# Ten of sixteen output projection blocks in half precision, and three attention pieces that begin one or two ticks later, in a hand-ordered layer kernel

## The chip, the cores and the metric

The kernel runs on one core of one Trainium2 chip. The metric is the device time of one execution in microseconds (us), as the median of several runs. The core has a matrix engine (TensorE, PE in the profile; its weight loads are listed as PEld), a vector engine (VectorE, DVE), an activation engine (ScalarE, ACT), a general engine (GpSimd, POOL), a sync engine (SyncE, SP) that issues most DMAs, an on-chip memory (SBUF) with 128 partitions, and a small memory for products (PSUM).

## The reference

One layer of a streaming encoder handles T = 320 tokens (a prompt of 256, and 64 sample tokens that also see 256 cached ones). The width D is 2048. All data and weights are float32.

```python
xn   = rmsnorm(x, norm_mix)
q, k, v, u, vs, g = split(xn @ w_in)          # 8 heads x 128 each for q, k, v; 1024, 1024; 4096
a    = stick_breaking(q, k, v)                # the sample tokens also see cache_k, cache_v
bb   = gelu(u) * (w_spatial @ rmsnorm(gelu(vs)) + b_spatial)
g_a, g_b = split(sigmoid(g + b_gate))
merged = g_a * (a @ w_branch_a) + g_b * (bb @ w_branch_b)
h    = x + merged @ w_out                     # the output projection, 2048 x 2048
gu   = rmsnorm(h, norm_ffn) @ w_gate_up       # FFN of width 5632
y    = rmsnorm(h + (silu(gu[:, :5632]) * gu[:, 5632:]) @ w_down, norm_final)
```

`stick_breaking` takes scores z = q.k / sqrt(128), forms log sigmoid(-z), sums it from the right along the keys, and weighs the values by exp(log sigmoid(z) + that sum). So each head has scores, a softplus, a scan, an exponential and a second product. The outputs are y and the new k, v and normalised vs.

## The kernel before, in words

Features lie on the partitions: an activation tile is 128 features x 320 tokens, and a matrix is walked in *blocks* of 128 output columns with 16 tiles of 128 inputs each. TensorE does not multiply float32 directly here. Weights and activations are each split into a high and a low part, and `product` (lines 104 to 106) issues three matmuls for each of the 16 tiles: high by high, high by low and low by high. A block is thus 48 matmuls of 320 columns into one PSUM buffer.

There are two ways to split. `Plain` keeps both parts in a 4-byte format (float32r): ScalarE casts the high part (`high`, line 126), VectorE subtracts to get the low part or *rest* (`low`, line 129), in two halves of 1024 columns each. `Group` uses 2-byte parts (float16). Since that format has a small range, the raw block is measured first: `bound` takes for each partition the sum of magnitudes on ScalarE (line 206) or, if the block is named in `by_vector`, the maximum on VectorE (line 202). `pack` (line 214) narrows it, `spread` (line 218) has TensorE broadcast it over partitions into the one `row` PSUM buffer, `close` (lines 222 to 224) takes the peak and makes powers of two `up` and `down`, `high` (line 356) casts raw x up, `low` (line 359) forms the rest, and the product is multiplied by `undo` when it is read. `Acts` does the same for a set of activation tiles: each tile's maximum when it is added, then pack, spread and close one, two and three ticks after the last tile, and from then on three tiles per tick are split by `half` (ScalarE line 166, VectorE line 167 a tick later).

A *tick* is half a block on TensorE. The other engines' steps are put into a table by tick (`at`, `after`) and issued by `rank` within the tick, low ranks first, each time `block` calls `tick`. So the order of instructions on every engine but GpSimd is what this table makes of it; each engine works its list strictly in that order. Before a block that starts at tick s, a `Plain` loads at s-8 and s-7, casts at s-2 and s-1, and takes the rests at s-1 and s. A `Group` (lead 11) loads at s-11 and s-10, bounds at s-8 (rank 4), packs at s-7 (rank 3), spreads at s-5 and closes at s-4 (rank 1), casts at s-3 and takes the rest at s-2 (rank 2). There are 5 raw buffers and 3 split buffers of one block each.

The stages are, in order: a start whose first heads are computed as the weights arrive; 6 `Plain` blocks (heads); then `line`, the list of half precision groups (4 gates, the other 12 heads, 8 blocks vs, 8 blocks u, 6 gates, and 16 branch blocks "ab" with gates between); the output projection `outs`, 16 `Plain` blocks that read the merged tiles as float32r pairs `mh`, `ml`; and the FFN, whose first three gate/up pairs (6 blocks) are `Plain` and all others `Group`. While the output projection runs, each finished block is added to x (`residual`, line 1021), multiplied by the norm's gain and split (`gained`, lines 159 and 160), and squared on ScalarE (line 275) and summed on GpSimd (line 276). The FFN's own half precision input comes from `Features`: `measure`, `spread` and `close` bound the gains during the output projection, and `normed` multiplies two tiles per tick by the norm's factor, each then split by `half`.

Attention works on four *pieces* of two heads. `attend(p, now)` puts one piece's steps into the table, over 19 ticks: parts now+1, planes +2, scores +3 and +4 (TensorE), gathering +4 and +5, softplus +6 and +7, scan +8 and +9, exponential +10 and +11, transposing DMAs +13, joining +16 (`together`, line 581, with the rests of line 601 a tick later), and the second product `att_out` +19 (TensorE). The rests of `att_parts` and `att_past` (lines 601 and 616) are what the scores read. GpSimd takes some of them.

## Time and profile before

| | us |
|---|---|
| median of 3 runs | 1622.87 |
| the three runs | 1621.71, 1622.87, 1623.84 |
| profiled execution | 1620.54 |
| its span (first to last instruction) | 1618.7 |
| start and first heads, up to the first half precision block | 0 to 90.94 |
| half precision: heads, gates, branches | 90.94 to 624.83 |
| output projection | 624.83 to 737.69 |
| FFN and end | 737.69 to 1618.7 |

A busy share tells how much of the span an engine works, averaged over stages with different limits; which engine ends last is read stage by stage. A row of the waits gives the waiting engine, what it was about to make (tile and line), what it waited for, the total in us, the number of times, and the longest. A row of the windows gives a stretch of time, its length, then busy time with the number of instructions for the engine, and the clock granted to TensorE as a share of full speed (PEclk).

### The profile page before, as it was taken

How to read it: one execution, taken by the hardware profiler on the slowest of the kernel's cores; microseconds unless marked ns; L12 is line 12 of the kernel's file. 1: busy time of each engine (PE TensorE's matmuls, PEld its weight loads, DVE VectorE, ACT ScalarE, POOL GpSimd, SP SyncE). 2: the span in 40 equal slices, each digit the busy share in tenths (PEclk: the TensorE clock that was granted, in tenths of full speed). 3: DMA queues.
4: the chain of work that ended last, by engine and by line, in shares of the span. 5: the costliest groups of instructions: out<-in, count | busy, mean ns of one | idle time of the engine just before them, and what ended most of it. 6: DMA issues, size and time to landing. Idle time of an engine off the chain costs nothing.

```text
span 1618.7 us, 28003 instructions
## 1 busy us (share of the span) xinstructions
PE 1598.7 (99%) x11692; PEld 1225.4 (76%) x11692; DVE 1089.1 (67%) x1819; ACT 1004.5 (62%) x1119; POOL 65.3 (4%) x80
## 2 busy tenths in 40 slices
PE   9989999999999999999999999999999999999997
PEld 9967777777777778999777777777777777777775
DVE  6788987886566565547856568665555776555775
ACT  6578999768666653446665656445555754565662
POOL 0110112100000000111000000000000000000000
PEclk9999999999999999999999999999999999999999
DMA  8656765554444444557544444444444444444321
GB/s 302 206 165 197 218 184 152 168 165 164 167 159 156 157 159 154 170 170 247 182 157 157 156 158 166 167 168 169 162 157 157 156 156 157 159 164 144 134 79 65
DMA packets 100511, 268.34 MB, mean 166 GB/s; under 512 B 28992, under 2 KB 35392, under 8 KB 100384
## 3 DMA queue, kind: packets, MB, share of 16 engines
q1 hardware_dynamic: 97936, 261.36, 48.4%
q0 software_dynamic: 1312, 3.80, 0.7%
q8 instruction: 91, 1.49, 0.4%
q10 hardware_dynamic: 1136, 1.39, 0.2%
q14 instruction: 36, 0.29, 0.0%
HBM read 256.03 MB, written 5.51 MB: 162 GB/s over the span
## 4 chain that ended last, share of the span: by engine, by line
PE 86%; ACT 6%; DVE 5%; issue 2%; DMA 1%; SPq 0%; DVEq 0%; ACTq 0%
PE acc L105 27%; PE acc L104 27%; PE acc L106 27%; PE aux L451 2%; ACT w L356 1%; ACT junk L206 1%; DVE w L359 1%; DMA raw<-w_in 1%; DVE tops L202 1%; PE acc L451 1%; DVE half L167 1%; DVE w L129 0%; PE row L218 0%; DMA turned<-wp 0%; DVE wt L581 0%
## 5 line engine op out<-in xcount | busy, mean ns | idle before, releaser
L105 PE MATMUL acc<-half,w 128*128 128x320 f16 x3232 | 967.1, 299 | 1.0 <-DVE half L167 1.0
L104 PE MATMUL acc<-half,w 128*128 128x320 f16 x3232 | 967.3, 299 | 0.0
L106 PE MATMUL acc<-half,w 128*128 128x320 f16 x3232 | 967.1, 299 | 0.1
L356 ACT ACTIVATE w<-raw,up 128x2048 f16<-128x2048 f32 (+1 forms) x206 | 405.4, 1968 | 449.1 <-PE acc L106 440.0
L359 DVE SCALAR_TENSOR_TENSOR w<-raw,up,w 128x2048 f16<-128x2048 f32 (+1 forms) x206 | 474.9, 2305 | 182.9 <-ACT w L356 182.8
L106 PEld LDWEIGHTS <-w 128*128 128x128 f16 x3232 | 316.4, 98 | 124.7 <-issue 1.2
L104 PEld LDWEIGHTS <-w 128*128 128x128 f16 x3232 | 316.5, 98 | 124.3 <-issue 1.3
L105 PEld LDWEIGHTS <-w 128*128 128x128 f16 x3232 | 316.5, 98 | 117.7 <-issue 0.2
L206 ACT ACTIVATE junk<-raw 128x2048 uint8<-128x2048 f32 (+1 forms) x149 | 278.0, 1866 | 1.7 <-DMA raw<-w_in 1.7
L222 DVE TENSOR_REDUCE peak<-row 128x1 f32<-128x128 f32 x148 | 42.6, 288 | 182.3 <-PE row L218 182.2
L202 DVE TENSOR_REDUCE tops<-raw 128x1 f32<-128x2048 f32 (+1 forms) x57 | 127.7, 2240 | 0.5 <-DMA raw<-w_gu 0.5
L126 ACT CAST w<-raw 128x1024 fp32r<-128x1024 f32 x56 | 58.7, 1048 | 94.2 <-PE acc L106 78.2
L129 DVE TENSOR_TENSOR w<-raw,w 128x1024 fp32r<-128x1024 f32 x56 | 68.8, 1232 | 50.3 <-ACT w L126 50.3
L104 PE MATMUL acc<-mh,w 128*128 128x320 f32 x256 | 79.3, 310 | 0.0
L105 PE MATMUL acc<-ml,w 128*128 128x320 f32 x256 | 79.1, 309 | 0.0
L106 PE MATMUL acc<-mh,w 128*128 128x320 f32 x256 | 79.1, 309 | 0.0
L104 PEld LDWEIGHTS acc<-mh,w 128*128 128x128 f32 x256 | 48.1, 188 | 0.0
L105 PEld LDWEIGHTS acc<-ml,w 128*128 128x128 f32 x256 | 48.1, 188 | 0.0
L106 PEld LDWEIGHTS acc<-mh,w 128*128 128x128 f32 x256 | 48.0, 188 | 0.0
L104 PE MATMUL acc<-S,w 128*128 128x320 f32 x144 | 44.7, 310 | 0.0
L106 PE MATMUL acc<-S,w 128*128 128x320 f32 x144 | 44.5, 309 | 0.0
L105 PE MATMUL acc<-S,w 128*128 128x320 f32 x144 | 44.5, 309 | 0.0
(227 smaller groups left out, 1197.7 us busy)
## 6 DMA issues: line engine op xcount, KB each, us to landing
raw<-w_gu SPq DMA_DIRECT2D x176, 512.0 KB, 5.7
raw<-w_in SPq DMA_DIRECT2D x141, 512.0 KB, 4.8
raw<-w_down SPq DMA_DIRECT2D x80, 512.0 KB, 4.9
raw<-w_out SPq DMA_DIRECT2D x32, 512.0 KB, 4.1
raw<-w_a SPq DMA_DIRECT2D x16, 512.0 KB, 3.7
raw<-w_b SPq DMA_DIRECT2D x16, 512.0 KB, 4.7
raw<-w_down SPq DMA_DIRECT2D x16, 256.0 KB, 4.5
x<-xT SPq DMA_DIRECT2D x8, 320.0 KB, 7.8
```

The source lines that it names most:

```text
L104: nc.tensor.matmul(ps[:, :T], a, x[0], start=first, stop=False, skip_group_check=True)
L105: nc.tensor.matmul(ps[:, :T], a, x[1], start=False, stop=False, skip_group_check=True)
L106: nc.tensor.matmul(ps[:, :T], b, x[0], start=False, stop=last, skip_group_check=True)
L126: nc.scalar.copy(out=self.w[j][0], in_=self.raw[:, j * HALF * P : (j + 1) * HALF * P])
L129: nc.vector.tensor_tensor(out=self.w[j][1], in0=self.raw[:, j * HALF * P : (j + 1) * HALF * P], in1=self.w[j][0].bitcast(F32), op=ALU.subt ...
L167: after(1, lambda: nc.vector.scalar_tensor_tensor(out=x[:, 1], in0=src, scalar=factor, in1=x[:, 0], op0=ALU.mult, op1=ALU.subtract), rank=3)
L202: nc.vector.tensor_reduce(out=self.tops[:, i : i + 1], in_=src, axis=mybir.AxisListType.X, op=ALU.max, apply_absolute_value=True)
L206: nc.scalar.activation(out=junk, in_=src, func=AF.Abs, accum_out=self.tops[:, i : i + 1])
L222: nc.vector.tensor_reduce(out=top, in_=self.row[:, :P], axis=mybir.AxisListType.X, op=ALU.max)
L356: nc.scalar.activation(out=w[:, 0], in_=self.raw[u][:, : self.width[u]], func=AF.Copy, scale=self.scale.up)
L359: nc.vector.scalar_tensor_tensor(out=self.w[u][1], in0=self.raw.pop(u)[:, : self.width[u]], scalar=self.scale.up, in1=self.w[u][0], op0=AL ...
L451: nc.tensor.matmul(first[b][h][:, :T], w[:, (h * n + j) * P : (h * n + j + 1) * P], xs[c + j][i], start=not last and c + j + i == 0, stop= ...
```

## The change

The output projection's first 6 blocks stay `Plain`. Blocks 6 to 15 become `Group`s with lead 11: weights bounded (on VectorE where m%3 is 2, so three of the ten), and the merged tiles collected in a new set `whole = Acts(KD)`, so that each merged tile's maximum is taken as it is merged, and 16 tiles are split into float16 pairs at ticks 3 to 8 of the stage. The float32r pairs are still made. `residual` of those blocks multiplies by `undo` on the way.

`attend` begins two ticks later for pieces 0 and 1, one later for piece 2, and at the same tick for piece 3. The step `att_past`, which is put into the table apart from `attend`, stays where it was.

Which blocks of `line` are bounded by VectorE follows a new rule: none of the first four, from 4 to 32 those whose number leaves 1 or 3 when divided by 5, then none up to 40, and then every third. Before, it was every third throughout (by the column block for "in", by m for "ab"). In the FFN the first groups are no longer bounded by VectorE (`made > 6`).

Closings (`Group.close`, `Acts.close`, and the FFN's `Features.close`, which also moves from tick 8 to tick 7 of the output projection) get rank 0.5, ahead of the other steps of their tick but the loads. The FFN's `normed` steps are spread over 7 ticks instead of 8.

```diff
+WHOLE_OUT = 6
...
-            at(last + 7, self.close, late_undo, rank=1)
+            at(last + 7, self.close, late_undo, rank=0.5)
...
-                at(now + 3, self.close, rank=1)
+                at(now + 3, self.close, rank=0.5)
...
-    attend(0, base + 10)
+    attend(0, base + 12)
...
+        by_vector = (0,) if 4 <= i < 33 and i % 5 in (1, 3) or i > 40 and i % 3 == 2 else ()
         if kind == "in":
-            g = Group([[(w_in[n][:, j * HALF * P : (j + 1) * HALF * P], HALF) for j in range(2)]], start, lambda: [mixed.undo], 11,
-                      (0,) if i % 3 == 2 else ())
+            g = Group([[(w_in[n][:, j * HALF * P : (j + 1) * HALF * P], HALF) for j in range(2)]], start, lambda: [mixed.undo], 11, by_vector)
         else:
-            g = Group([[(w_a[n], H), (w_b[n], H)]], start, lambda: [aT.undo, bT.undo], 11, (0,) if n % 3 == 2 else (), True)
+            g = Group([[(w_a[n], H), (w_b[n], H)]], start, lambda: [aT.undo, bT.undo], 11, by_vector, True)
...
-    outs = [Plain(w_out[m], KD, out_start + 2 * m) for m in range(KD)]
+    whole = Acts(KD)
+    outs = [Plain(w_out[m], KD, out_start + 2 * m) for m in range(WHOLE_OUT)]
+    outs += [Group([[(w_out[m][:, j * HALF * P : (j + 1) * HALF * P], HALF) for j in range(2)]], out_start + 2 * m,
+                   lambda: [whole.undo], 11, (0,) if m % 3 == 2 else (), True) for m in range(WHOLE_OUT, KD)]
...
-            attend(1, state["tick"] + 9)
+            attend(1, state["tick"] + 11)
         elif name == "v" and h % 2:
-            attend(h // 2, state["tick"] + 1)
+            attend(h // 2, state["tick"] + (2 if h == 5 else 1))
...
+        whole.add(t)
...
-                groups[kind, s, i] = Group([pieces(w_gu[i], 0, KD), pieces(w_gu[KF + i], 0, KD)], now, lambda: [ffn.undo], min(14, now - ffn_start), (1,) if made % 2 else ())
+                groups[kind, s, i] = Group([pieces(w_gu[i], 0, KD), pieces(w_gu[KF + i], 0, KD)], now, lambda: [ffn.undo], min(14, now - ffn_start), (1,) if made % 2 and made > 6 else ())
...
-    at(out_start + 8, ffn.close)
+    at(out_start + 7, ffn.close, rank=0.5)
...
-        nc.vector.tensor_tensor(out=hs[m], in0=ps, in1=x, op=ALU.add)
+        if m < WHOLE_OUT:
+            nc.vector.tensor_tensor(out=hs[m], in0=ps, in1=x, op=ALU.add)
+        else:
+            nc.vector.scalar_tensor_tensor(out=hs[m], in0=ps, scalar=outs[m].undo, in1=x, op0=ALU.mult, op1=ALU.add)
...
-        ps = outs[m].block(merged)
+        ps = outs[m].block(merged) if m < WHOLE_OUT else outs[m].block(0, whole.half)
...
-        at(base + 3 + m // 2, lambda m=m: ffn.normed(m, hs[m], "rh", lambda: rooms["raw"].tile([P, T], F32, tag="normed", bufs=6, name="normed")))
+        at(base + 3 + 7 * m // 16, lambda m=m: ffn.normed(m, hs[m], "rh", lambda: rooms["raw"].tile([P, T], F32, tag="normed", bufs=6, name="normed")))
```

Line numbers after the change are one higher up to about line 800 and more behind it. The order of the engines' lists shows the moves. First VectorE at the scores of piece 0, where `S<-q` and `S<-k` are the rests that the scores read (the last is `128x2x64`, line 616 before and 617 after), `w<-raw,up,w` is a weight block's rest, and `peak`, `down`, `up`, `undo` are a closing. Before:

```order
L222 TENSOR_REDUCE peak<-row 128x1
L223 TENSOR_TENSOR down<-peak,bits 128x1
L224 TENSOR_TENSOR up<-down,bits 128x1
L349 TENSOR_SCALAR undo<-down,undo_610 128x1
L359 SCALAR_TENSOR_TENSOR w<-raw,up,w 128x2048
L601 TENSOR_TENSOR S<-q,S 128x256
L601 TENSOR_TENSOR S<-k,S 128x256 x2
L616 TENSOR_TENSOR S<-q,S 128x2x64
L757 TENSOR_TENSOR v<-acc,rx 128x320
```

After, the same place:

```order
L360 SCALAR_TENSOR_TENSOR w<-raw,up,w 128x2048
L758 TENSOR_TENSOR v<-acc,rx 128x320
L215 TENSOR_SCALAR packed<-tops 128x1
L223 TENSOR_REDUCE peak<-row 128x1
L224 TENSOR_TENSOR down<-peak,bits 128x1
L225 TENSOR_TENSOR up<-down,bits 128x1
L350 TENSOR_SCALAR undo<-down,undo_610 128x1
L360 SCALAR_TENSOR_TENSOR w<-raw,up,w 128x2048
L602 TENSOR_TENSOR S<-q,S 128x256
L602 TENSOR_TENSOR S<-k,S 128x256 x2
L617 TENSOR_TENSOR S<-q,S 128x2x64
```

The rests of piece 0 now stand behind one more closing and one more weight rest, and behind the reading of a head v that followed them before.

On GpSimd, the three subtractions of piece 0's cached keys (`S<-k,S 128x320 x3`) and a memset of 512 columns stand like this before:

```order
L759 DMA k_t<-k 128x320
L528 MEMSET wso 128x512
L535 DMA wso<-ws_t 64x4x64 x2
L601 TENSOR_TENSOR S<-k,S 128x320 x3
L759 DMA v_t<-v 128x320
```

And after:

```order
L760 DMA k_t<-k 128x320
L602 TENSOR_TENSOR S<-k,S 128x320 x3
L529 MEMSET wso 128x512
L536 DMA wso<-ws_t 64x4x64 x2
L760 DMA v_t<-v 128x320
```

The subtractions come ahead of the memset.

Second, VectorE where piece 2 is joined (`wt<-turned`) and the scores of piece 3 are gathered (`z<-aux,mdiag`). Before:

```order
L581 COPY wt<-turned 128x2x640
L581 COPY wt<-turned 128x2x512
L222 TENSOR_REDUCE peak<-row 128x1
L223 TENSOR_TENSOR down<-peak,bits 128x1
L224 TENSOR_TENSOR up<-down,bits 128x1
L349 TENSOR_SCALAR undo<-down,undo_610 128x1
L359 SCALAR_TENSOR_TENSOR w<-raw,up,w 128x2048
L202 TENSOR_REDUCE tops<-raw 128x1
L658 TENSOR_TENSOR z_2883<-aux,mdiag 128x2x128
```

After:

```order
L223 TENSOR_REDUCE peak<-row 128x1
L224 TENSOR_TENSOR down<-peak,bits 128x1
L225 TENSOR_TENSOR up<-down,bits 128x1
L350 TENSOR_SCALAR undo<-down,undo_610 128x1
L360 SCALAR_TENSOR_TENSOR w<-raw,up,w 128x2048
L203 TENSOR_REDUCE tops<-raw 128x1
L582 COPY wt<-turned 128x2x640
L582 COPY wt<-turned 128x2x512
L659 TENSOR_TENSOR z_2881<-aux,mdiag 128x2x128
```

The joining of piece 2 has come to stand in the same tick as the gathering for piece 3 and directly ahead of it.

Third, VectorE in the output projection around the fifth and sixth tick, where `w<-raw,w 128x1024` is half a `Plain` block's rest, `h<-acc,ev` a residual and `S<-h,gain,S` a gained rest. Before:

```order
L129 TENSOR_TENSOR w<-raw,w 128x1024
L1021 TENSOR_TENSOR h<-acc,ev 128x320
L160 SCALAR_TENSOR_TENSOR S<-h,gain,S 128x320
L129 TENSOR_TENSOR w<-raw,w 128x1024 x2
L1021 TENSOR_TENSOR h<-acc,ev 128x320
L160 SCALAR_TENSOR_TENSOR S<-h,gain,S 128x320
```

After:

```order
L130 TENSOR_TENSOR w<-raw,w 128x1024
L1027 TENSOR_TENSOR h<-acc,ev 128x320
L215 TENSOR_SCALAR packed<-tops 128x1
L168 SCALAR_TENSOR_TENSOR half<-gate,act_up,half 128x320 x3
L161 SCALAR_TENSOR_TENSOR S<-h,gain,S 128x320
L223 TENSOR_REDUCE peak<-row 128x1
L224 TENSOR_TENSOR down<-peak,bits 128x1
L225 TENSOR_TENSOR up<-down,bits 128x1
L130 TENSOR_TENSOR w<-raw,w 128x1024
L168 SCALAR_TENSOR_TENSOR half<-gate,act_up,half 128x320 x3
L203 TENSOR_REDUCE tops<-raw 128x1
```

Between two residuals there are now the rests of three merged tiles per tick, a closing and, once, a block's maximum.

## The prediction

> **What bounds the kernel now.** I read the page's first two parts, then busy time by windows for TensorE, then its waits, then the groups of instructions by line and shape, and last the timeline around each wait.
>
> ```profile
> span 1618.7 us, 28003 instructions
> PE 1598.7 (99%) x11692; PEld 1225.4 (76%) x11692; DVE 1089.1 (67%) x1819; ACT 1004.5 (62%) x1119; POOL 65.3 (4%) x80
> ```
>
> TensorE (PE) is busy 99% of the span, so time can only come from a faster matmul or from its few waits. The windows below are, in order: the 16 output projection blocks; 30 plain half precision blocks (gates and branches); two blocks with the scores of attention piece 1 in them; one block with the output of piece 0; the block that holds the scores of piece 0; the five blocks in which piece 3 ends; the first half precision block of the FFN.
>
> ```profile
> core 0: us, PE busy (x), PEclk, DMA share, GB/s
> 624.83:737.69 112.86, 112.86 (x771) 1.00 0.53 166
> 408.10:605.37 197.27, 197.27 (x1472) 1.00 0.47 161
> 132.72:147.69 14.97, 14.97 (x115) 1.00 0.98 245
> 154.26:163.18 8.92, 8.92 (x72) 1.00 0.35 118
> 90.94:106.40 15.46, 10.40 (x65) 0.78 0.64 194
> 256.87:297.16 40.29, 37.44 (x268) 0.96 0.64 180
> 780.18:788.01 7.83, 6.87 (x51) 1.00 0.28 107
> ```
>
> A float32r block takes 112.86/16 = 7.05 us, a half precision one 197.27/30 = 6.58 us (its bound's broadcast matmul included), so a tick (half a block) is 3.52 or 3.29 us. Scores add 14.97 - 2 x 6.58 = 1.8 us, an output piece 8.92 - 6.58 = 2.3 us. What is left over is waiting:
>
> - **A**, scores of piece 0: 15.46 - 6.58 - 1.8 = 7.1 us
> - **B**, end of piece 3: 40.29 - 5 x 6.58 - 2.3 = 5.1 us
> - **C**, start of the FFN: 7.83 - 6.58 = 1.25 us
>
> ```profile
> PE aux L629 <- DVE S L616: 5.1, 1, 5.1
> PE row L218 <- DVE peak L222: 1.5, 3, 0.8
> PE aux L721 <- DVE S L601: 1.3, 1, 1.3
> PE acc L105 <- DVE half L167: 1.0, 1, 1.0
> PE aux L721 <- ACT S L600: 0.6, 1, 0.6
> ```
>
> These are TensorE's own waits (us in total, times, longest): A is the first, B the 1.3, the 0.6 and half of the 1.5, C the 1.0. Everywhere else the other engines' waiting costs nothing.
>
> **The change, part by part: attention.** Around A the timeline shows VectorE (DVE), GpSimd (POOL) and TensorE:
>
> ```profile
> 92.74 3.11 DVE L224 TENSOR_TENSOR up<-down,bits 128x1 int32<-128x1 int32 x1
> 95.89 2.33 DVE L359 SCALAR_TENSOR_TENSOR w<-raw,up,w 128x2048 f16<-128x2048 f32 x1
> 99.16 0.28 DVE L616 TENSOR_TENSOR S<-q,S 128x128 fp32r<-128x128 f32 x1
> ...
> 93.32 2.50 POOL L601 TENSOR_TENSOR S<-k,S 128x320 fp32r<-128x320 f32 x3
> ...
> 102.34 0.47 PE L104 MATMUL acc<-half,w 128*128 128x320 f16 x1
> 102.61 0.47 PE L105 MATMUL acc<-half,w 128*128 128x320 f16 x1
> 103.34 0.30 PE L105 MATMUL acc<-half,w 128*128 128x320 f16 x1
> 103.48 0.30 PE L106 MATMUL acc<-half,w 128*128 128x320 f16 x1
> ```
>
> TensorE stood until 99.4, when the last rest of piece 0 was done; the matmuls after it start 0.27 us apart instead of 0.14 until 103.3, which is part of the 7.1. Without the wait the scores would have begun at 99.4 - 5.1 = 94.3; two ticks later that is 94.3 + 2 x 3.29 = 100.9. VectorE has one weight rest (2.3), one closing of a bound and two small steps more before that point, some 3.5 us, and, since group 2's bound goes to ScalarE (ACT), one reduction of 2.3 us less, of which up to all is lost waiting for ScalarE. So the rest is ready between 99.4 + 3.5 - 2.3 = 100.6 and 102.9: a wait of 0 to 2.0 us, and no slow clock. I take 0.8, nearer the lower end, because the 3.11 us step (0.18 us as a rule, by its row further down) goes with GpSimd's three subtractions, which now come ahead of their memset and so fall earlier. A gains 6.3.
>
> B is different, for there ScalarE is the bound. Windows from the gathering of piece 2 to that of piece 3, and on to the end of piece 3 (PE, PEld, DVE, ACT, POOL):
>
> ```profile
> 191.31:234.87 43.56, 43.56 (x331) 32.54 (x329) 35.87 (x71) 40.93 (x54) 4.10 (x6) 1.00 0.72 196
> 234.87:290.17 55.30, 52.45 (x385) 38.81 (x383) 43.37 (x80) 48.72 (x61) 14.43 (x8) 0.98 0.53 152
> ```
>
> ScalarE works 40.9 of 43.6 us. Pieces 0 and 1 start two ticks later, piece 2 one, piece 3 at the same tick: from 1 to 2 and from 2 to 3 it is now 11 ticks instead of 12. A tick less takes 3.3 us of time away and only about 1.9 us of ScalarE's work (half a high part of 2.0 us, half of 0.6 bounds at 1.9 and a readout, 0.3 for reading a product), so each interval loses 1.4 us of slack. The removed A gives nothing here; it was TensorE's slack. Also the joining of piece 2 now stands ahead of the gathering for piece 3 in the same tick:
>
> ```profile
> L581 DVE COPY wt<-turned 128x1280 uint16<-128x1280 uint16 x4 | 3.6, 891 | 0.0
> L581 DVE COPY wt<-turned 128x1024 uint16<-128x1024 uint16 x4 | 3.0, 738 | 0.0
> ```
>
> That is 1.6 us of VectorE. Against that, the bound at the tick of group 28 moves from ScalarE to VectorE (2.1 us off the engine that is late), and group 29's goes the other way. So B becomes 5.1 - 2.0 = 3.1 at best, 5.1 + 2 x 1.4 + 1.6 = 9.5 at worst; I take 6.5, one interval's loss. A and B together: 12.2 - 0.8 - 6.5 = **4.9 gained**, between 0.7 (2.0 and 9.5 left) and 9.1 (0 and 3.1 left).
>
> **Output projection.** Ten blocks go from 7.05 to 6.58: 10 x 0.478 = 4.8 us, less one broadcast matmul for the bound of the merged tiles (under 0.1): 4.7. Prices of what is added, from the groups by shape (busy us, mean ns):
>
> ```profile
> L359 DVE SCALAR_TENSOR_TENSOR w<-raw,up,w 128x2048 f16<-128x2048 f32 x190 | 445.9, 2347 | 178.0 <-ACT w L356 178.0
> L356 ACT ACTIVATE w<-raw,up 128x2048 f16<-128x2048 f32 x190 | 380.2, 2001 | 416.1 <-PE acc L106 407.0 <-PE row L218 2.5 <-DVE undo L349 2.5
> L206 ACT ACTIVATE junk<-raw 128x2048 uint8<-128x2048 f32 x137 | 260.4, 1901 | 1.7 <-DMA raw<-w_in 1.7
> L202 DVE TENSOR_REDUCE tops<-raw 128x1 f32<-128x2048 f32 x53 | 120.7, 2277 | 0.5 <-DMA raw<-w_gu 0.5
> L129 DVE TENSOR_TENSOR w<-raw,w 128x1024 fp32r<-128x1024 f32 x56 | 68.8, 1232 | 50.3 <-ACT w L126 50.3
> L126 ACT CAST w<-raw 128x1024 fp32r<-128x1024 f32 x56 | 58.7, 1048 | 94.2 <-PE acc L106 78.2 <-issue 10.4 <-PE aux L451 4.9
> L167 DVE SCALAR_TENSOR_TENSOR half<-act,act_up,half 128x320 f16<-128x320 f32 x44 | 21.5, 544 | 0.0
> L276 POOL TENSOR_TENSOR sq_h<-sq_h,sq 128x320 f32<-128x320 f32 x14 | 14.8, 1061 | 389.9 <-ACT sq L275 389.9
> L160 DVE SCALAR_TENSOR_TENSOR S<-h,gain,S 128x320 fp32r<-128x320 f32 x16 | 11.7, 739 | 5.5 <-ACT S L159 5.5
> L160 DVE SCALAR_TENSOR_TENSOR S<-x,gain,S 128x320 fp32r<-128x320 f32 x8 | 4.1, 548 | 4.7 <-ACT S L159 4.6
> L224 DVE TENSOR_TENSOR up<-down,bits 128x1 int32<-128x1 int32 x148 | 26.5, 179 | 5.1
> L222 DVE TENSOR_REDUCE peak<-row 128x1 f32<-128x128 f32 x148 | 42.6, 288 | 182.3 <-PE row L218 182.2
> ```
>
> Splitting costs no more than before (one high part of 2.0 us for two casts of 1.05, one rest of 2.35 for two of 1.23). New are ten bounds (seven on ScalarE at 1.9 and a readout that I put at 0.2, three on VectorE at 2.3) and 16 merged tiles' halves and rests. In the later blocks this is hidden: ScalarE 2.0 + 2.1 + 1.0 and VectorE 2.35 + 0.8 + 1.3 lie under 6.58. The full place is ticks 3 to 8 of the stage, 6 x 3.52 = 21.1 us. VectorE has there six weight rests (7.4), 15 halves' rests (8.2), three closings (2.6), three residuals (at a half's rest) and two gained rests (3.1), a reduction for block 8 (2.3), packings (0.6): 24.2. ScalarE has six casts (6.3), 16 high halves (about as long as their rests, 8.7), two bounds (4.2), three pairs of gained and square (1.0 each): 22.2. The next weight rest must be done 7 ticks after the start, at 24.6, and would end at 24.2 + 1.2 = 25.4. The 30 or so rows overlap their neighbours by up to 0.06 us each, which could bring it down to 23.6. So TensorE waits 0 to 0.8 there; VectorE being late also delays the closing of a bound that a broadcast waits for, and a raw buffer that is asked for one tick before it is free. I take 1.0, bounds 0 to 3. Net **3.7 gained**, between 1.7 and 4.7.
>
> The longer matmul hides nothing now: in half precision a block leaves 0.47 us less to the engines beside it, which is in the 6.58 already.
>
> Here a rule speaks against the change. GpSimd adds one square per block; rests beside it took 739 instead of 548 ns, 0.19 us more. The Trainium skill (SBUF — State Buffer, section "SBUF: two separate sides") says that VectorE and GpSimd share a port pair as an exclusive lock, and whoever starts second is blocked for the whole instruction; the 3.11 us step at 92.74 agrees. By it the three adds of those six ticks would cost VectorE up to 3.2 us instead of 0.6.
>
> **FFN.** All normalised tiles are ready one tick earlier, and two reductions (4.6 us) leave VectorE for ScalarE before C. VectorE's list up to the last rest shrinks from about 31 to 27 us, while the wait was 1.25. ScalarE gets 4.2 us in two ticks with slack around them. C gains **1.2**, bounds 0 and 1.25. Closing bounds ahead of equal work in a tick moves steps of 0.2 to 0.8 us within VectorE's queue; I cost it at nothing, with 0.7 either way (the remaining 0.7 of the waits for the peak).
>
> **The rivals.**
>
> 1. Attention's waits go altogether: the bound moved off ScalarE at piece 3 is enough and A fits. Gain 12.2 + 3.7 + 1.2 = 17.1, 1605.8 us. Against it stand the 94% of ScalarE. Chance 0.12.
> 2. GpSimd's adds hold VectorE for their whole length in the output projection: 24.2 + 3.2 + 1.2 = 28.6 against 24.6, a wait of 4.0 instead of 1.0. Gain 9.8 - 3.0 = 6.8, 1616.1 us. For it speaks one step of 3.11, against it the 739. This is the lock rule's case. Chance 0.08.
> 3. Half precision is no faster there, or the blocks are fed too late throughout: gain 4.9 + 1.2 - 1.0 = 5.1, 1617.8 us. The 30 blocks speak against it. Chance 0.05.
> 4. Slower: the squeezed pieces do not shrink with the ticks, because their steps wait for each other. A rest of piece 1 (then 2) now stands on VectorE behind the maximum of the next piece, which waits for ScalarE's logarithm:
>
> ```profile
> DVE e L672 <- ACT e L667: 9.1, 4, 2.8
> ```
>
> Then both lost ticks come back as waits (6.6), both outputs wait 2.8, and each long wait brings the slow clock of A again (1.8 each): B is 5.1 + 6.6 + 5.6 + 3.6 = 20.9, A 2.0, so 10.7 lost against 4.9 gained elsewhere: 1628.7 us. It decides from B over 18 us on. Chance 0.06.
>
> My own case has 0.69.
>
> **How the numbers follow.** 4.9 + 3.7 + 1.2 = 9.8 us. The profiled execution took 1620.5 us (span 1618.7) and would take 1610.7; the median of the runs is 1622.9, 2.4 above it, and all differences come from gaps that do not depend on that, so I predict 1622.9 - 9.8 = **1613.1 us**. My case alone reaches from a gain of 15.1 (9.1 + 4.7 + 1.25) to one of 2.4 (0.7 + 1.7 + 0): 1607.8 to 1620.5. The range, with most of rival 1, is 1606 to 1620.5. A change under 0.2%, 3.2 us, can't be told from none here. My case falls short of that in about one of 20, rival 3 in one of five: faster 0.87, same 0.07, slower 0.06.
>
> **What would show it.** Output blocks 6 to 15 at 6.58 us and a wait under 1 us near the sixth; TensorE's wait at L616's successor under 2.0 us with the clock at 1.00; the wait for the rests of piece 3 still there, 3 to 9 us with ScalarE over 90% busy; none on the halves at the FFN. I am wrong if B goes to nothing or over 10, or if TensorE waits over 3 us in the output projection.

## The result, and the profile after

The changed kernel takes 1610.52 us (median of 6 runs, 1610.40 to 1612.64) against 1623.36 (median of 6, 1621.71 to 1624.23): a ratio of 0.9924, 95% interval 0.9911 to 0.9936. It is faster by 12.8 us. The forecast was 1613.1, with a range of 1606 to 1620.5. One execution of the kernel before, beside the later experiments, took 2790.15 us at a mean granted clock of 0.556, and no number below uses it.

The two profiled executions differ by less, 1620.54 and 1610.42 us (spans 1618.7 and 1608.6): 10.1 us. The remaining 2.7 us are taken up further down. The page of the changed kernel:

```profile
span 1608.6 us, 28118 instructions
PE 1591.9 (99%) x11703; PEld 1201.1 (75%) x11703; DVE 1126.9 (70%) x1905; ACT 1016.0 (63%) x1131; POOL 68.1 (4%) x80
```

TensorE is still the bound, so the question is again which of its waits went and which came. Its waits now (total, times, longest):

```profile
PE aux L630 <- DVE S L617: 1.6, 1, 1.6
PE row L219 <- DVE peak L223: 1.3, 3, 0.5
PE aux L722 <- DVE S L602: 1.1, 1, 1.1
PE acc L107 <- DVE w L360: 1.1, 1, 1.1
PE acc L105 <- DVE ev L1063: 1.0, 1, 1.0
```

The first two rows look like old waits that shrank. The first is not: it stands before the scores of another piece. Windows cut at the same blocks show where the 10.1 us come from. First the kernel before, in this order: the block with the scores of piece 0 and the next; the two blocks with the scores of piece 2; the seven blocks around the end of piece 3; the last eight branch blocks; the output projection; the FFN's six plain blocks; the six behind them.

```profile
90.94:112.99 22.05, 16.99 (x114) 0.85 0.59 174
176.33:191.31 14.98, 14.98 (x114) 1.00 1.03 304
256.87:310.74 53.87, 50.81 (x367) 0.97 0.65 181
572.49:624.83 52.34, 52.34 (x392) 1.00 0.44 145
624.83:737.69 112.86, 112.86 (x771) 1.00 0.53 166
737.69:780.18 42.49, 42.49 (x293) 1.00 0.79 265
780.18:820.72 40.54, 39.58 (x293) 1.00 0.51 177
```

The same blocks of the changed kernel:

```profile
90.68:105.65 14.97, 14.97 (x115) 1.00 0.62 207
169.00:185.82 16.82, 15.17 (x115) 1.00 1.00 247
251.46:302.37 50.91, 49.24 (x367) 1.00 0.68 190
564.12:619.08 54.96, 53.14 (x391) 1.00 0.42 139
619.08:727.56 108.48, 108.48 (x783) 1.00 0.55 175
727.56:771.31 43.75, 42.77 (x292) 1.00 0.69 242
771.31:810.61 39.30, 39.30 (x293) 1.00 0.55 193
```

Length is the first number behind the stretch. Gained: 7.1 at the scores of piece 0, 3.0 at the end of piece 3, 4.4 in the output projection, 1.2 at the FFN's first half precision block. Lost: 1.8 at the scores of piece 2, 2.6 in the last branch blocks, 1.3 in the FFN's plain blocks. With 0.3 us from the start the sum is 10.2, against 10.1 of the spans; all other stretches agree within 0.1.

### The profile page after: what moved, and what is told of

It is laid out like the page before. It is cut to its first block, busy times and chain, and to the rows that moved or that the text cites. A ratio compares the mean times of both kernels' runs of the same rounds, so it can differ in the third digit from the quotient of the medians.

```text
span 1608.6 us, 28118 instructions
## 1 busy us (share of the span) xinstructions
PE 1591.9 (99%) x11703; PEld 1201.1 (75%) x11703; DVE 1126.9 (70%) x1905; ACT 1016.0 (63%) x1131; POOL 68.1 (4%) x80
## 4 chain that ended last, share of the span: by engine, by line
PE 90%; ACT 5%; DVE 3%; issue 1%; DMA 0%; DVEq 0%; POOL 0%; ACTq 0%
PE acc L105 29%; PE acc L107 29%; PE acc L106 29%; PE aux L452 2%; ACT w L357 1%; PE acc L452 1%; DVE w L360 1%; ACT junk L207 1%; DVE tops L203 1%; PE row L219 1%; DMA bsb<-bs 0%; ACT S L601 0%; ACT L667 0%; DVE h L1179 0%; PE row L416 0%
## 5 line engine op out<-in xcount | busy, mean ns | idle before, releaser
L107 PE MATMUL acc<-half,w 128*128 128x320 f16 x3392 | 1014.2, 299 | 1.2 <-DVE w L360 1.1
L105 PE MATMUL acc<-half,w 128*128 128x320 f16 x3392 | 1014.3, 299 | 0.4 <-DVE gate L967 0.3
L106 PE MATMUL acc<-half,w 128*128 128x320 f16 x3392 | 1014.2, 299 | 0.0
L357 ACT ACTIVATE w<-raw,up 128x2048 f16<-128x2048 f32 (+1 forms) x216 | 425.3, 1969 | 470.8 <-PE acc L107 465.8
L360 DVE SCALAR_TENSOR_TENSOR w<-raw,up,w 128x2048 f16<-128x2048 f32 (+1 forms) x216 | 499.0, 2310 | 190.8 <-ACT w L357 190.8
L107 PEld LDWEIGHTS <-w 128*128 128x128 f16 x3392 | 331.9, 98 | 130.6 <-DVE w L360 1.8
L105 PEld LDWEIGHTS <-w 128*128 128x128 f16 x3392 | 331.9, 98 | 130.5 <-issue 1.5
L106 PEld LDWEIGHTS <-w 128*128 128x128 f16 x3392 | 331.9, 98 | 123.7 <-issue 0.9
L127 ACT CAST w<-raw 128x1024 fp32r<-128x1024 f32 x36 | 37.6, 1044 | 41.1 <-PE acc L107 29.5
L130 DVE TENSOR_TENSOR w<-raw,w 128x1024 fp32r<-128x1024 f32 x36 | 44.4, 1235 | 4.0 <-ACT w L127 3.9
L1078 DVE SCALAR_TENSOR_TENSOR h<-acc,undo,h 128x320 f32<-128x320 f32 x47 | 25.7, 547 | 16.2 <-PE acc L107 16.2
L219 PE MATMUL row<-turner,packed 128*128 128x128 bf16 x159 | 34.9, 220 | 1.4 <-DVE peak L223 1.3
L277 POOL TENSOR_TENSOR sq_h<-sq_h,sq 128x320 f32<-128x320 f32 x14 | 18.1, 1290 | 385.6 <-ACT sq L276 385.6
L105 PE MATMUL acc<-mh,w 128*128 128x320 f32 x96 | 30.2, 315 | 0.0
```

The costliest lines, as they stand in the source:

```text
L105: nc.tensor.matmul(ps[:, :T], a, x[0], start=first, stop=False, skip_group_check=True)
L106: nc.tensor.matmul(ps[:, :T], a, x[1], start=False, stop=False, skip_group_check=True)
L107: nc.tensor.matmul(ps[:, :T], b, x[0], start=False, stop=last, skip_group_check=True)
L127: nc.scalar.copy(out=self.w[j][0], in_=self.raw[:, j * HALF * P : (j + 1) * HALF * P])
L130: nc.vector.tensor_tensor(out=self.w[j][1], in0=self.raw[:, j * HALF * P : (j + 1) * HALF * P], in1=self.w[j][0].bitcast(F32), op=ALU.subt ...
L219: nc.tensor.matmul(self.row[:, :P], self.own.to_broadcast([P, P]), turner, start=True, stop=True)
```

## The experiments

Twelve kernels gave a time, nearly all of them the changed kernel with one part undone. A thirteenth, with all three edits at the FFN's start undone together (first bounds, closing of the gains, normalised tiles), deadlocks and has no time. "Scores of piece 0", "end of piece 3" and so on are the stretches above. Each stretch is read from one profile per kernel, and the medians are given beside it.

**Attention's pieces at their old ticks.**

```diff
-    attend(0, base + 12)
+    attend(0, base + 10)
...
-            attend(1, state["tick"] + 11)
+            attend(1, state["tick"] + 9)
...
-            attend(h // 2, state["tick"] + (2 if h == 5 else 1))
+            attend(h // 2, state["tick"] + 1)
```

> The changed kernel with attention's pieces begun at the old ticks, all else as changed. If the scores of piece 0 gained by beginning later (my theory), their block takes 13 to 15.5 us again instead of 8.4: 5 to 7 us lost; the new wait before the scores of piece 2 (1.8 us) goes, since the maximum that stands before their rests falls behind them. If the gain at the end of piece 3 (2.9 us) comes from which engine takes the bounds, it stays here, and the sum is 1610.5 + 7.1 - 1.8 = about 1615.8 us. Rival: the pieces' new spacing made that gain; then another 2.9 is lost, about 1618.7 us.

Measured: 1617.15 us (1615.98 to 1619.97). The scores of piece 0 take 21.4 us again, those of piece 2 15.0 without a wait, the end of piece 3 49.8, even 1.1 less than in the changed kernel. But 2.6 us are lost between, among them a new wait of 1.5 us before the scores of piece 3. The gain at the end of piece 3 does not come from the spacing.

**The old choice of bounds on VectorE.** The code of this edit also shows that the old choice went by a group's place in `line` (by m for "ab"), not by the column block. The groups are numbered by that place.

```diff
-        by_vector = (0,) if 4 <= i < 33 and i % 5 in (1, 3) or i > 40 and i % 3 == 2 else ()
+        by_vector = (0,) if (i if kind == "in" else n) % 3 == 2 else ()
```

> The changed kernel with the old choice of blocks of the line that VectorE bounds, all else as changed. By my theory ScalarE is late again at the end of piece 3, with the pieces closer together: 2.9 us or more lost there (up to 7, as the prediction's 9.5 us of waiting would have it); the scores of piece 2 lose their new wait of 1.8; the scores of piece 0 keep their gain but for 0 to 2 us; the branch blocks keep their 2.6 us of waiting, because that hangs on a buffer and not on VectorE's load. Sum: 1611 to 1617 us. Rival: the branch blocks wait because VectorE now bounds most of them; then those 2.6 us go here, and the sum is 2.6 less.

Measured: 1619.7 us (1617.5 to 1621.2), above what I expected. The branch blocks keep their 2.6 us, as expected. The end of piece 3 takes 52.7, so 1.8 are lost there. But the scores of piece 0 take 19.3 us and those of piece 2 19.0: I had expected at most 2 us lost at the first, and a gain at the second. VectorE at piece 0, where TensorE waits for line 617:

```profile
97.55 2.34 DVE L360 SCALAR_TENSOR_TENSOR w<-raw,up,w 128x2048 f16<-128x2048 f32 x1
99.81 2.28 DVE L203 TENSOR_REDUCE tops<-raw 128x1 f32<-128x2048 f32 x1
102.00 0.41 DVE L602 TENSOR_TENSOR S<-q,S 128x256 fp32r<-128x256 f32 x1
102.34 0.75 DVE L602 TENSOR_TENSOR S<-k,S 128x256 fp32r<-128x256 f32 x2
103.01 0.28 DVE L617 TENSOR_TENSOR S<-q,S 128x128 fp32r<-128x128 f32 x1
```

The maximum of line 203 is that of group 5. With the old choice it falls in the same tick as the rests and is ranked ahead of them.

**The same, with the rests ahead of a maximum.** The old choice as above, and the rests for the scores get rank 3.5 instead of 5 (a bound has 4). `parts` gets an argument `rank=5` for it, and uses it for its rest.

```diff
-        s["qp"] = parts(s["q"][:, :, P:TP])
-        s["kp"] = [parts(s["k"][:, j, 0:TP]) for j in range(2)]
+        s["qp"] = parts(s["q"][:, :, P:TP], rank=3.5)
+        s["kp"] = [parts(s["k"][:, j, 0:TP], rank=3.5) for j in range(2)]
...
-        after(1, lambda: nc.vector.tensor_tensor(out=own[:, :, 1], in0=new, in1=own[:, :, 0].bitcast(F32), op=ALU.subtract))
+        after(1, lambda: nc.vector.tensor_tensor(out=own[:, :, 1], in0=new, in1=own[:, :, 0].bitcast(F32), op=ALU.subtract), rank=3.5)
```

> The changed kernel with the old choice of bounds on VectorE, and with the rests for the scores put ahead of a block's maximum in the same tick. With the old choice alone the scores' blocks took 12.7 us (piece 0) and 12.4 us (piece 2). Theory: at piece 0 TensorE waits because one maximum of 2.3 us (group 5's) stands right before the rests; ahead of it they are ready 2.3 us earlier, and without the long wait the slow matmuls go too: 8.4 to 9.3 us, some 3.5 to 4.3 gained. At piece 2 no maximum stands there; ScalarE is late with two bounds in a row, and the block stays at 12 to 12.6 us. Sum: 1619.7 - 4 = about 1615.7 us. Rival: at both places it is the load of VectorE and ScalarE that counts and not the order; then both blocks change by under 1 us, 1619 us or above.

Measured: 1615.81 us (1615.29 to 1618.41), as expected. VectorE at the same place:

```profile
99.76 0.42 DVE L602 TENSOR_TENSOR S<-q,S 128x256 fp32r<-128x256 f32 x1
100.10 0.75 DVE L602 TENSOR_TENSOR S<-k,S 128x256 fp32r<-128x256 f32 x2
100.77 0.28 DVE L617 TENSOR_TENSOR S<-q,S 128x128 fp32r<-128x128 f32 x1
100.97 2.27 DVE L203 TENSOR_REDUCE tops<-raw 128x1 f32<-128x2048 f32 x1
```

The same work in another order: the rests end 2.2 us earlier, and the block takes 8.8 us instead of 12.7. At piece 2, where no maximum stands ahead and VectorE waits 2.5 us for a cast of ScalarE just before the rests, nothing changes (12.4).

**Both old.** The pieces at their old ticks and the old choice of bounds together; the rests keep their rank.

> The changed kernel with both the pieces' old starts and the old choice of bounds on VectorE. It completes a table of four: from the first half precision block to the end of piece 3 (29 blocks) the kernel before took 219.9 us, the changed one 211.7, with the old starts 218.0, with the old choice 220.4. Theory: these two edits alone make the 8.1 us, and only together; closings moved ahead count for nothing there. Then it takes 219.9 us: 1610.5 + 8.1 = 1618.6 us. Rival: the closings' new rank made part of it; then the stretch takes 216 to 219 us, 1615 to 1617.5 us.

Measured: 1620.84 us (1618.45 to 1623.49), profiled 1620.02. That is 2.2 us above the forecast in the median. The 29 blocks take 221.0 us, 1.2 more than before the change; 0.9 of it are at piece 0, after the same long wait. So the closings' rank alone does not make the gain, and the table of four is:

| 29 blocks, us | old choice of bounds | new choice |
|---|---|---|
| old starts | 221.0 | 217.9 |
| later starts | 220.3 | 211.7 |

Later starts alone gain 0.6, the choice alone 3.1, both 9.3. By the medians of the whole kernels the same steps are 1.1, 3.7 and 10.3.

**The closings' old rank.**

```diff
-            at(last + 7, self.close, late_undo, rank=0.5)
+            at(last + 7, self.close, late_undo, rank=1)
...
-                at(now + 3, self.close, rank=0.5)
+                at(now + 3, self.close, rank=1)
```

> The changed kernel with the closings of groups and of activation sets at their old rank, all else as changed. Theory: steps of 0.2 to 0.8 us within VectorE's queue, nothing: 1610.5 us within 0.7, as the prediction has it. Rival: without them a broadcast waits longer for its peak where VectorE is busiest, at piece 3 and at the branch blocks' end: 1 to 2 us lost, 1611.5 to 1612.5 us.

Measured: 1610.57 us (1610.39 to 1610.76). No difference, as the prediction had it.

**Other buffers for three gates.** The new waits in the branch blocks hang on ScalarE. Its list in the changed kernel:

```profile
564.32 2.00 ACT L357 ACTIVATE w<-raw,up 128x2048 f16<-128x2048 f32 x1 [1.91 <-PE acc L107]
578.31 0.53 ACT L840 ACTIVATE gate<-acc,undo 128x320 f32<-128x320 f32 x1 [11.99 <-PE acc L107]
578.74 1.90 ACT L207 ACTIVATE junk<-raw 128x2048 uint8<-128x2048 f32 x1
...
581.53 3.88 ACT L357 ACTIVATE w<-raw,up 128x2048 f16<-128x2048 f32 x2
```

A gate's reading waits 12 us "for PE acc". The product that it reads was done at 564.1, when its block ended, so the wait is for something else that TensorE releases. The buffers' addresses in the built program tell: the gate's tile gets the slot of a normalised tile (`half`), which TensorE reads for the last time in the last gate block, from 577.7 on. Before the change that gate got the slot of a gate long merged, and 42 of the 51 slots were in use. Now all 51 are, since the merged tiles stay until the output projection splits them. The next weight cast, due when a block ends at 571.1, comes 10 us late.

```diff
-        gt = gate[m, i] = slot(dt=F32, name="gate")
+        spare = {(14, 1): "bb", (15, 0): "mg", (15, 1): "bb"}.get((m, i))
+        gt = gate[m, i] = t320(spare, 1 if spare == "mg" else 2) if spare else slot(dt=F32, name="gate")
```

> The changed kernel with the last three gate tiles kept in other buffers than the 51 shared slots. My theory: in the changed kernel a gate's reading on ScalarE stands 12 us until the last gate block on TensorE has read a normalised tile, whose slot the gate gets, since the 16 merged tiles now hold slots until the output projection. With other buffers that wait goes and the branch blocks take 52.3 us again instead of 55.0: 1610.5 - 2.6 = 1607.9 us. Rival: VectorE's maxima of the merged tiles and of the blocks make these waits; then nothing changes, 1610.5 us.

Measured: 1608.12 us (1607.88 to 1609.69). The branch blocks take 52.33 us, as before the change. The same gate (its tile is now named `bb`) is read at once:

```profile
564.87 2.00 ACT L357 ACTIVATE w<-raw,up 128x2048 f16<-128x2048 f32 x1 [1.91 <-PE acc L107]
566.78 0.51 ACT L841 ACTIVATE bb<-acc,undo 128x320 f32<-128x320 f32 x1
```

**Output projection plain again.**

```diff
-WHOLE_OUT = 6
+WHOLE_OUT = 16
...
-        whole.add(t)
```

> The changed kernel with all 16 output projection blocks plain again, and so without the set of merged tiles; all else as changed. If half precision alone makes the gain in that stage (my theory), it takes 112.9 us instead of 108.5, and the branch blocks lose their 2.6 us of waiting, because no merged tile holds a slot: 1610.5 + 4.4 - 2.6 = 1612.3 us. So ten half precision blocks are worth 1.8 us net as they were put in. The new wait of 1.2 us in the FFN's plain blocks stays. Rival: that wait comes from the output projection's work for VectorE running over; then it goes as well, 1611.1 us.

Measured: 1612.4 us (1612.17 to 1612.46). The stage takes 112.87 us, the branch blocks 52.33; the wait in the FFN's plain blocks stays (8.33 us for that block). So half precision in the output projection was worth 4.4 - 2.6 = 1.8 us as it was put in.

**The first FFN bounds on VectorE again**, and, in a kernel of its own, **two normalised tiles per tick again**:

```diff
-                groups[kind, s, i] = Group([pieces(w_gu[i], 0, KD), pieces(w_gu[KF + i], 0, KD)], now, lambda: [ffn.undo], min(14, now - ffn_start), (1,) if made % 2 and made > 6 else ())
+                groups[kind, s, i] = Group([pieces(w_gu[i], 0, KD), pieces(w_gu[KF + i], 0, KD)], now, lambda: [ffn.undo], min(14, now - ffn_start), (1,) if made % 2 else ())
```

> The changed kernel with the first FFN bounds on VectorE again, all else as changed. Theory: ScalarE's two bounds one behind the other make VectorE wait for them (2.7 and 0.7 us) before it reads the plain product for which TensorE waits; with one of each pair on VectorE, that wait of 1.2 us goes, and the later wait for halves of normalised tiles returns with 0 to 1.2 us: 1609.3 to 1610.5 us. Rival: VectorE's own load makes it; then the two reductions of 2.3 us add to it, the wait grows to 3 us or more, and the time is 1612.5 us or above.

Measured: 1609.29 us (1609.27 to 1609.50).

```diff
-        at(base + 3 + 7 * m // 16, lambda m=m: ffn.normed(m, hs[m], "rh", lambda: rooms["raw"].tile([P, T], F32, tag="normed", bufs=6, name="normed")))
+        at(base + 3 + m // 2, lambda m=m: ffn.normed(m, hs[m], "rh", lambda: rooms["raw"].tile([P, T], F32, tag="normed", bufs=6, name="normed")))
```

> The changed kernel with two normalised tiles per tick again (eight ticks instead of seven), all else as changed. Theory: the third tile in two of the ticks makes VectorE late at the plain product; with two per tick that wait falls from 1.2 to under 0.5 us, and the wait for the halves at the first half precision block returns with up to 1.2 us: 1610 to 1611 us. Rival: the spreading has nothing to do with it; then 1.2 stays and another 1.2 comes: 1611.7 us.

Measured: 1609.66 us (1609.43 to 1609.86). The plain block that took 8.33 us takes 7.16 in the first and 7.41 in the second; the half precision block behind takes 6.68 and 6.59. VectorE's first wait in these stages of the changed kernel is this one:

```profile
DVE topmost L213 <- ACT junk L207: 3.4, 2, 2.7
```

With the bounds back on VectorE this row is gone. Up to the reading for which TensorE waits, only one of the two maxima (2.28 us) had left VectorE's list, and 3.4 us of waiting for ScalarE's sums had come. With two tiles per tick the row stays (3.8 us), but VectorE takes fewer normalised tiles ahead of that reading. So either edit taken back removes most of the new wait, and the old wait for the halves hardly returns. What took that one away is then the gains' earlier closing, or the two edits each for itself; the closing was not tried alone, so this stays open.

**Rests ahead of a maximum, on top of the other buffers.** All rests of attention's parts get rank 3.5.

> The kernel with the gates in other buffers (1608.1 us), and the rests of attention's parts put ahead of a block's maximum in the same tick (rank 3.5 instead of 5). Theory: TensorE waits for the scores of piece 2 because VectorE takes a maximum of 2.3 us right before the rests; ahead of it they are ready in time: 1.8 us gained there, and up to 1.3 us at the end of piece 3: 1605.0 to 1606.3 us. Rival: VectorE and ScalarE are simply late there by their load; then what is moved behind is waited for instead, and the time stays at 1608 us or rises.

Measured: 1606.30 us (1606.20 to 1607.07), the upper end. The scores of piece 2 take 15.0 instead of 16.8; the end of piece 3 takes 51.3, 0.4 more than in the changed kernel. So the new order is not free: by these stretches it gains 1.9 us and costs 0.4. In the changed kernel the maximum at piece 2 stands right ahead of the rests, as group 5's stood at piece 0 with the old choice:

```profile
177.16 2.28 DVE L203 TENSOR_REDUCE tops<-raw 128x1 f32<-128x2048 f32 x1
179.36 0.41 DVE L602 TENSOR_TENSOR S<-q,S 128x256 fp32r<-128x256 f32 x1
179.69 0.75 DVE L602 TENSOR_TENSOR S<-k,S 128x256 fp32r<-128x256 f32 x2
180.36 0.28 DVE L617 TENSOR_TENSOR S<-q,S 128x128 fp32r<-128x128 f32 x1
```

**All together, and with one half precision block more.** The first takes the other buffers, the rests first (for scores and joined weights) and the FFN's bounds on VectorE; the second has `WHOLE_OUT = 5` as well.

> The changed kernel with the last three gate tiles in other buffers, the rests for scores and for the joined weights (not those of the joined values) ahead of a block's maximum, and the first FFN bounds on VectorE again. Theory: the three gains lie in different places and add: 2.6 + 1.85 + 1.05 = 5.5 us, and 0.6 more at the end of piece 3, where the rests of the joined values no longer delay a bound: 1610.5 - 6.1 = 1604.4 us. Rival: they don't add, since each moves work on VectorE into the next stage: 1606 us or above.

> The same with eleven half precision blocks in the output projection instead of ten. Theory: one more block gains 0.46 us (7.04 against 6.58), and VectorE has 0.6 us of room at the sixth block: 1603.9 us. Rival: the merged tiles' halves and the block's own weights meet in one tick more, VectorE is late, and TensorE waits 1 to 3 us there: 1605 to 1607 us.

Measured: 1605.5 us (1605.31 to 1605.89; ratio to the kernel before 0.9891, interval 0.9875 to 0.9908) and 1605.19 us (1604.81 to 1606.00; 0.9889, 0.9875 to 0.9904). The gains at piece 2, the branch blocks and the FFN add up; the 0.6 us hoped for at the end of piece 3 did not come (51.3 us), and 0.4 was lost there, so the first lies 1.1 us above its forecast. One more half precision block takes 0.45 us off the stage, as forecast (0.46), without a new wait in it; but the runs of the two kernels overlap, and their times alone do not tell them apart.

Both are about 5 us faster than the changed kernel and 18 faster than the one before. Of TensorE's waits the longest left in both is 1.1 us, at the end of piece 3.

## Why the prediction was right, and where it was wrong

The total was close, 9.8 us forecast against 10.1 between the two profiled executions, and the direction was right. But the terms were less good than their sum, for errors of both signs cancelled: that the sum came so close is luck.

**Scores of piece 0 (6.3 forecast, 7.1 measured): right in mechanism and size, with the wrong group named.** The prediction had a later start bring more of VectorE's work ahead of the rests, one maximum less to pay for it, and the slow clock gone. TensorE reaches the scores at 100.56 (100.9 worked out) and finds the rests done at 100.20 (100.6 to 102.9 worked out):

```profile
99.91 0.29 DVE L617 TENSOR_TENSOR S<-q,S 128x128 fp32r<-128x128 f32 x1
100.56 0.82 PE L630 MATMUL aux<-S 128*128 128x320 f32 x4
```

But the maximum that mattered was group 5's, which the later start moves the rests behind, and not group 2's: with the old choice, and so with group 2's maximum still on VectorE, the block took 8.8 us once the order was changed, against 8.4 in the changed kernel. The 3.11 us step is gone too, as expected with GpSimd's subtractions ahead of its memset:

```profile
89.92 3.04 POOL L602 TENSOR_TENSOR S<-k,S 128x320 fp32r<-128x320 f32 x3 [7.71 <-issue]
89.53 1.63 DVE L168 SCALAR_TENSOR_TENSOR half<-x,gain,half 128x320 f16<-128x320 f32 x2
91.09 1.15 DVE L602 TENSOR_TENSOR S<-k,S 128x320 fp32r<-128x320 f32 x1
```

VectorE still pays beside them, 0.6 and 0.7 us in these rows (two such halves took 1.01 right before, and the same rest 0.48 in the kernel with both parts old), but earlier, where it has time.

**End of piece 3 (1.4 lost by forecast, 3.0 gained): wrong, outside even the bounds given for it.** In the windows, 1.4 of the 3.0 us are waits (53.87 - 50.81 = 3.06 before, 50.91 - 49.24 = 1.67 after). The other 1.6 are TensorE's busy time (50.81 and 49.24): in the kernel before, matmuls ran at half the clock here. The prediction counted its 5.1 us at B as waiting, though the waits that it lists for B come to some 2.7; it named the slow clock at A alone. The same stretch with both parts old, with the old starts, and with the old choice of bounds:

```profile
257.82:311.97 54.15, 51.07 (x366) 0.97 0.64 180
259.20:309.04 49.84, 48.75 (x366) 1.00 0.67 189
258.46:311.18 52.72, 49.45 (x367) 1.00 0.65 185
```

Length less busy time is 3.1, 1.1 and 3.3 us of waiting. So the later starts cost 0.2 us of waiting with the old choice and 0.6 with the new one, and the new choice takes 2.0 us of waiting away with the old starts and 1.6 with the later ones. The step that failed is "each interval loses 1.4 us of slack": both intervals and the joining together cost 1.1 us in length at most (49.8 to 50.9). The choice of bounds, the prediction's "2.1 us off the engine that is late", did what its best case allowed (2.0), and the prediction took nothing of it. The joining ahead of the gathering was not tried alone.

**Scores of piece 2 (nothing forecast, 1.8 lost): missed.** The prediction looked at A and B because the kernel before waited there. The later start moves piece 2's rests into the tick of group 16's bound, and the new choice makes that bound a maximum on VectorE. It takes both for this wait: with the old starts the two blocks take 15.0 us, and with the later start and the old choice another wait stands there, 2.2 us, for ScalarE. The same look at the order as for piece 0 would have shown it.

**Output projection (3.7 forecast, 4.4 measured in the stage, 1.8 net): right where it looked.** Half precision blocks take 6.4 to 6.6 us. The full ticks 3 to 8 brought no wait of TensorE, but the six plain blocks take 42.99 us instead of 42.46, with five broadcast matmuls among theirs instead of one: 0.5 us of the 1.0 set aside. The failed step is "16 merged tiles' halves and rests", which was counted as work alone: the work was hidden, but the tiles hold their slots until these ticks, and an engine that works strictly in order stood 12 us for one. A sum of durations does not show that.

**FFN (1.2 forecast, 0 measured): the wait named went, and another of the same size came** two blocks earlier. The prediction said of ScalarE that it gets "4.2 us in two ticks with slack around them". VectorE's packing stands behind these sums and waited 3.4 us for them, so the slack was not there.

**The median (9.8 forecast, 12.8 measured).** The prediction put the same difference on the median as on the profile, since gaps "do not depend on that". The runs speak against that. The runs of the five kernels with a wait of over 2 us before scores spread over 3 to 7 us (1618.45 to 1623.49 with both parts old; 1619.12 to 1625.97 for the kernel before); the runs of each of the other nine lie within 0.2 to 2.3 us. The profiled execution of the kernel before was one of its faster ones.

**The rivals.** The waits did not all vanish (1.), half precision was faster (3.), and the pieces did not come late (4.). GpSimd's lock (2.) shows, but did not decide: in ticks 3 to 8 two of its adds fell, one of them made a half's rest of VectorE 0.6 us longer (1.17 instead of 0.54), and TensorE did not wait there. Over the stage it cut both ways, by which of the two began first:

```profile
659.89 0.88 POOL L277 TENSOR_TENSOR sq_h<-sq_h,sq 128x320 f32<-128x320 f32 x1 [8.10 <-ACT sq L276]
660.14 0.98 DVE L161 SCALAR_TENSOR_TENSOR S<-h,gain,S 128x320 fp32r<-128x320 f32 x1
667.82 2.35 DVE L360 SCALAR_TENSOR_TENSOR w<-raw,up,w 128x2048 f16<-128x2048 f32 x1 [0.64 <-ACT w L357]
668.67 2.22 POOL L277 TENSOR_TENSOR sq_h<-sq_h,sq 128x320 f32<-128x320 f32 x1 [1.83 <-ACT sq L276]
```

The rest that began behind the add took 0.98 us instead of 0.54, and the add that began behind a weight rest took 2.22 instead of 0.88. After the change few of VectorE's rests begin behind an add, so by the mean they became shorter (0.61 us instead of 0.74) and the adds longer (1.29 instead of 1.06).

## What to carry to other kernels

When work is handed to another engine or begun later, look at the order in every tick where a waited-for step falls, not only where the old waits were: one maximum of 2.3 us ahead of 1.4 us of rests cost 3.9 us at piece 0 (1.9 of it slow matmuls behind the wait) and 1.8 at piece 2, and a rank took that away, for 0.4 us lost later. When a tile must live longer, count the buffers as well as the work; a reading that waits for an engine long done with its product was waiting here for a buffer. Two edits of a schedule need not add: in these profiles later starts gave 0.6 us, the choice of bounds 3.1, both 9.3.

## What the runs showed of the hardware that I had not expected

TensorE runs slowly after a wait that is not even long. Here are two stretches of the kernel with the old choice of bounds, the blocks with the scores of pieces 0 and 2, and then two parts of the first, cut where the recorded clock changes (length, TensorE's busy time, granted clock):

```profile
97.44:110.13 12.69, 10.26 (x66) 0.87 0.75 229
180.05:192.46 12.41, 10.24 (x66) 0.86 0.98 250
100.45:103.86 3.41, 0.98 (x8) 1.00 1.01 382
103.86:107.27 3.41, 3.41 (x15) 0.50 0.20 78
```

The waits were 2.4 and 2.2 us. Behind them the matmuls of the scores ran slowly, and then 11 and 8 others, 0.27 us apart instead of 0.136. Without a wait these blocks take 8.38 us (changed kernel) and 8.39 (rests first), all of it busy; here TensorE is busy 10.26 and 10.24. So 1.9 us are lost in each beside the wait, and a wait of 2.2 us costs 4.0.

After waits of 4.8 to 5.3 us there were 6, 9 and 14 slow matmuls. After a wait of 1.65 us there were none; after 1.3 us at the end of piece 3 there were 3 and 6 in two kernels and none in two others. The counts differ, but each of the eight slow stretches in these profiles lasts 3.41 us, or 6.83 after two of the long waits; what is lost depends on how much of it falls into the wait itself. In the 3.41 us just ahead of each, TensorE had been idle for 1.4 us or more: for 2.4 us in the third row. When the fourteen profiles are cut into stretches of 3.41 us from one change of the clock on, the clock fell behind each of the seven at full speed in which TensorE was idle for 1.9 us or more, and behind one of the five with 1.4 to 1.7 us. What decides there was not found. That the cost is not the same in each run fits the spread of the runs above; that the spread comes from this alone was not shown.

The Trainium skill (TensorE: Matmul & The Clock Gate, section "Part 1: The HAM clock gate (the "warmup" mystery)") tells of a free-running window of about 3.4 us and says that the count of slow matmuls differs from run to run. The traces agree as far as they go: the changes of the clock lie whole multiples of 3.41 us apart in each profile (107.27 to 185.78 is 23 times), and the counts differ between kernels. It gives one idle window of about 3.4 us as the condition; here 2.2 us were enough.
